# Regrouping the second norm's tiles, and placing the late lists' row numbers ahead of gates and factors

## The chip, the cores and the metric

One program runs on one core of a Trainium2 chip. The metric is the device time of an execution in microseconds (us); lower is better. Engines are named as in the profile: PE is TensorE, DVE is VectorE, ACT is ScalarE, POOL is GpSimd, SP is SyncE, which here only issues DMAs. All times in the text are from the start of the profiled execution's span.

## The reference, cut to what matters

A decoder layer over 2048 tokens of width 1024. Its last two parts are touched here. `h` is the output of the first norm:

```python
zg = xt @ w_rg + b_rg                      # 4 groups
pg = softmax(zg); gsel = argmax(zg)
ze = (xt @ w_re + b_re)[chosen group]      # 8 experts in the group
top_v, top_i = top_k(ze, 2)
gate = pg[gsel] * softmax(top_v)           # the factor of each choice
eid = gsel * 8 + top_i                     # which of 32 experts
...
hid = silu(xb @ w_gate[e]) * (xb @ w_up[e])
y  += gate * (hid @ w_down[e])             # summed per token
out = layer_norm(ALPHA * h + y, ln2_g, ln2_b)
```

## The kernel before, in words

**Stages.** A first long stage computes both mixers and merges them. The projection stage then runs over pairs of tiles (`p` from 0 to 7, two tiles of 128 tokens each): output projection on TensorE, first norm on VectorE, then routing. The expert stage goes through 32 experts in order: tokens are gathered by row number from `hd` (the normed rows in HBM), turned by TensorE, multiplied, and added to `acc` in HBM by an indirect DMA from GpSimd. Last comes the second norm, over `acc`. Instructions run on each engine in the order in which the program issues them (`manual_schedule`); an engine that waits holds everything behind it in its own queue.

**Routing of a pair.** `logits` and `gather_logits` bring the scores to PSUM through turned tiles (`hturn`). `route1` (line 1133 on) takes the maxima, makes `ef` (the expert's number), the one-hot `oh` and `ob`, and then the factor `sd` out of two sigmoids (`sp_`, `sm_`) and the gate `gt`: six small VectorE operations behind `ob`. `rank` has TensorE count, with five short matmuls, how many earlier tokens chose the same expert. `route2` makes the rank `rk` and from it `sl`, the row of an HBM table `td`; `scatter` writes token number and factor there, by four indirect DMAs of GpSimd.

**The late lists.** The last two pairs (6 and 7, `late` = 0 and 1) don't go through the table. The lists of the others are read early (`early_lists`), and the late ones are added by matmuls: `place` (line 1257) writes a one-hot `o` of the rank and, per choice, two selections `m` of the list, one with the token's number and one with its factor: twelve operations per pair, three per choice. `place_sum` multiplies `o` with both halves of `m` at once (192 columns) into one PSUM tile. The sums are added to the early lists as `TF` (row numbers) and `TG` (factors).

**Order of the hand-over** (lines 1379 to 1411, the text around the change):

```python
norm(p, (1,))              # last tile; p = 7
high(0, 2, 3); early_lists()
route2(p - 1, rank(p - 1)) # places pair 6
hturn(2 * p + 1)           # TensorE turns the last tile
logits(p, 1); gather_logits(p)
place_sum(0)
early_rows(); low(0, 2); load(2, 0, (0,))
ascale(p - 1); route1(p)
route2(p, rank(p))         # places pair 7
place_sum(1); low(0, 3); load(2, 0, (1,))
...                        # TF, TG, counts
```

`high` and `low` split a quarter of an expert's weights into a rounded and a rest part, on ScalarE and VectorE (1.2 us a piece). Behind this come `TI` (TF as integers), the first gather of expert 0's rows into `X1`, `select` (row numbers `NX` of the next blocks), the counts' register loads (`table`), the second gather, `select_last`, low(0, 4, 5), low(1, 0, 1), and `turn(X1)`: TensorE turns X1, ScalarE copies its high half, VectorE writes its low half (`bhl`). `gateup` multiplies per step high with high, high with low and low with high, so its third matmul needs VectorE's half.

**The second norm** (lines 1662 to 1769). `F` holds six groups of 2, 2, 4, 2, 4 and 2 tiles. `moments` takes a group's mean and variance on ScalarE (a summing read and a summing square per tile), `moments_v` on VectorE with its norm statistics; groups 0 and 3 go to VectorE, 1, 2, 4 and 5 to ScalarE. `root` is eleven small VectorE operations per group (a reciprocal root by Newton's steps), the first of which, `f_v`, reads the variance. `scale1` and `scale2` are one large VectorE operation each per tile. `POOL` names one tile each in groups 1 to 4 that GpSimd does whole: three operations and its own write. `weave` alternates one small operation of a group's `root` with one large one of `scale2` of the group before and `scale1` of its own.

Of the kernel before, what the change touches and what calls it, by code (L numbers as in the profile page):

```python
# [13 lines left out]
I32 = mybir.dt.int32  # L14
# [71 lines left out]
def layer(ctx, tc, a, out, dbg=None):  # L86
# [808 lines left out]
    spacer = rc_.tile([1, 1], F32, name="spacer")  # L895

    TF = rc_.tile([128, NE + 1, JB], F32, name="tf")
    TG = rc_.tile([128, NE, JB], F32, name="tg")
# [237 lines left out]
    def route1(p):  # L1136
# [27 lines left out]
        A.activation(gt[:, :, 1], dv, AF.Sigmoid, scale=-1.0)  # L1164
        ef = small("r_ef", [2, 2])
        V.tensor_copy(ef, j8[:, :, 0:2])
# [4 lines left out]
        ob = small("r_ob", [2, 32], BF16)  # L1171
        V.tensor_tensor(ob, oh[:, :, 0, :], oh[:, :, 1, :], op=OP.add)
        V.reciprocal(sm_, sm_)
        V.tensor_tensor(sp_, sp_, sm_, op=OP.mult)
# [5 lines left out]
        V.tensor_copy(sd[:, :, :, 0], tokid[:, 2 * p:2 * p + 2].unsqueeze(2).to_broadcast([128, 2, 2]))  # L1180
        RT_[p] = (ef, oh, ob, sd)

    def rank(p):
        ef, oh, ob, sd = RT_[p]
        pk = paux([128, 2, 32])
        PE.matmul(pk[:, 0, :], tri, ob[:, 0, :], start=True, stop=False)
        PE.matmul(pk[:, 0, :], onb, ohs, start=False, stop=True)
        PE.matmul(pk[:, 1, :], tri, ob[:, 1, :], start=True, stop=False)
        PE.matmul(pk[:, 1, :], onb, ob[:, 0, :], start=False, stop=False)
        PE.matmul(pk[:, 1, :], onb, ohs, start=False, stop=True)  # L1190
        return pk

    def route2(p, pk):
        ef, oh, ob, sd = RT_.pop(p)
        for t in range(2):
            V.tensor_tensor(ohs, ohs, ob[:, t, :], op=OP.add)
        V.tensor_tensor(oh, oh, pk.unsqueeze(2).to_broadcast([128, 2, 2, 32]), op=OP.mult)

        rk, sl = small("r_rk", [2, 2]), rc_.tile([128, 2, 2], I32, name="r_sl", bufs=2)
        V.tensor_reduce(rk, oh, axis=AX.X, op=OP.add)  # L1200
        dv = oh[:, :, :, 0]
        late = p - NP + 2
        if late >= 0:
            place(late, rk, ef, oh, sd)
        V.tensor_scalar(dv, rk, 1.0 / 128.0, -0.498, op0=OP.mult, op1=OP.add)
# [3 lines left out]
        V.scalar_tensor_tensor(sl, rk, 16.0, dv, op0=OP.mult, op1=OP.add)  # L1209
        if late >= 0:  # L1210
            SLD.append((sl, sd))
        else:
            scatter(sl, sd)

    SLD = []

# [15 lines left out]
    def late_buffers():  # L1232
# [11 lines left out]
        V.tensor_scalar(tv, tokid[:, NT - 4:NT], -float(EMPTY), None, op0=OP.add)  # L1244
        LB.extend([o, m, te, tf, io, tv, ps_, pmm([128, 2, NL])])

    LB = []

    def early_lists():
        te, tf = LB[2:4]  # L1250
        A.dma_start(te.rearrange("p (e c) -> p e c", e=NE), dap(td, 0, [[1024, 128], [32, NE], [1, 2 * JB]]))

    def early_rows():
        te, tf = LB[2:4]
        V.tensor_copy(tf, te.rearrange("p (n c) -> p n c", c=2)[:, :, 0])

    def place(l, rk, ef, oh, sd):
        o, m, te, tf, io, tv, ps_, pt = LB
# [8 lines left out]
        for c in range(4):  # L1267
            V.tensor_scalar(o[:, l, c], io, rm[:, c:c + 1], None, op0=OP.is_equal)
            V.tensor_scalar(m[:, l, c, 0], io[:, 0:NL], eb[:, c:c + 1], tv[:, 2 * l + c // 2:2 * l + c // 2 + 1],
                            op0=OP.is_equal, op1=OP.mult)  # L1270
            V.tensor_scalar(m[:, l, c, 1], io[:, 0:NL], eb[:, c:c + 1], sd[:, c // 2, c % 2, 1:2].bitcast(F32),
                            op0=OP.is_equal, op1=OP.mult)

    def place_sum(l):
        o, m, te, tf, io, tv, ps_, pt = LB
        for c in range(4):
            PE.matmul(pt.rearrange("p v n -> p (v n)"), o[:, l, c], m[:, l, c].rearrange("p v n -> p (v n)"),
                      start=l == 0 and c == 0, stop=l == 1 and c == 3)

# [50 lines left out]
    for p in range(NP):  # L1330
# [47 lines left out]
        if p == NP - 3:  # L1378
# [14 lines left out]
    gather_logits(p)  # L1393
    place_sum(0)
    early_rows()
    low(0, 2)
    load(2, 0, (0,))
    ascale(p - 1)
    route1(p)
    route2(p, rank(p))  # L1400
    place_sum(1)
    low(0, 3)
    load(2, 0, (1,))
    pc = paux([128, 32])
    PE.matmul(pc, onb, ohs, start=True, stop=True)
    V.tensor_tensor(TF[:, 0:NE].rearrange("p e b -> p (e b)"), LB[-1][:, 0], LB[3], op=OP.add)
    V.tensor_tensor(TG.rearrange("p e b -> p (e b)"), LB[-1][:, 1],
                    LB[2].rearrange("p (n c) -> p n c", c=2)[:, :, 1].bitcast(F32), op=OP.add)
    ascale(p)
    V.tensor_copy(cnt[:, 0:32], pc[0:1, :])  # L1410
# [170 lines left out]

    gather(X1, TI[:, 0, 0:1])
    high(1, 2, 3, 4, 5)
# [53 lines left out]
    with tc.If(mx > 128 * JB):  # L1637
        for sl, sd in SLD:
            scatter(sl, sd)
        with tc.For_i(0, NE, 1) as e:  # L1640
# [22 lines left out]
    F, i = [], 0  # L1663
    for n in (2, 2, 4, 2, 4, 2):
        f = bigt([128, n, D], F32, "f")
# [32 lines left out]

    POOL = {1: 1, 2: 3, 3: 1, 4: 3}

# [54 lines left out]

    for k in (1, 2, 4, 5):
        moments(k)
# [4 lines left out]
    weave([scale2(1)], iter(()))  # L1762
    moments_v(3)
    weave([scale1(2)], root(2))
# [27 lines left out]
```

## Time and profile before

| | us |
|---|---|
| median of 3 runs | 1833.65 (1828.17 to 1834.74) |
| the profiled execution | 1831.52 |
| its span, first to last instruction | 1829.8 |
| busy: TensorE, VectorE, ScalarE, GpSimd | 1710.9, 1324.6, 695.7, 304.9 |

The span is what the traces show; the execution's own time has 1.7 us around it. A row of a timeline gives start, duration, engine, line, operation, output and inputs with their shapes, and in brackets how long the engine had been idle before it and what ended that. Most rows have the line of a helper (L66), so the names of the tiles tell which operation it is: `late` is the buffer of `o` and `m`, `aux` a small PSUM tile, `rg` the rows of the first norm, `pt` the turned rows of a gather, `pg` the result of `gateup`.

### The profile page before, as it was taken

What the parts mean: (1) busy time and instruction counts of PE and PEld (TensorE: products, weight loads), DVE (VectorE), ACT (ScalarE), POOL (GpSimd) and SP (SyncE); (2) the same over time, 40 slices, a digit from 0 to 9 for tenths busy, and PEclk for the clock granted to TensorE, in tenths of its full rate; (3) what the DMA queues carried; (4) which work ended last, traced back from release to release, by engine and by line L of the source; (5) the groups of instructions that cost most, each with busy time, mean ns of one, the idle gap of its engine ahead of it and who ended that gap; (6) DMA issues with size and microseconds to landing.
All of it is one profiled execution on the core that took longest, in us unless ns stands there. A gap on an engine that the chain in (4) does not pass through costs nothing. (4 is left out here: it accounts for less than half of the span.)

```text
span 1829.8 us, 23985 instructions
## 1 busy us (share of the span) xinstructions
PE 1710.9 (94%) x8384; PEld 1374.7 (75%) x8385; DVE 1324.6 (72%) x2463; ACT 695.7 (38%) x1069; POOL 304.9 (17%) x304
## 2 busy tenths in 40 slices
PE   8999999999999999999999999994999999999930
PEld 7888877777777778777788888883778787887720
DVE  5798787768877875765575678898765556667748
ACT  5111221222222222633330122225776556667743
POOL 2000001101101101000000011221334333333415
PEclk9999999999999999999999999996999999999975
DMA  7321432432342325333463432546988878889855
GB/s 221 93 93 46 116 85 68 151 93 80 99 129 97 95 85 198 114 115 112 156 240 112 147 116 93 191 138 224 305 263 267 268 205 255 262 269 322 246 182 228
DMA packets 213755, 300.80 MB, mean 164 GB/s; under 512 B 29119, under 2 KB 159249, under 8 KB 211041
## 3 DMA queue, kind: packets, MB, share of 16 engines
q1 hardware_dynamic: 166496, 213.32, 35.5%
q0 software_dynamic: 22896, 56.06, 11.2%
q10 hardware_dynamic: 24208, 29.47, 4.8%
q8 instruction: 86, 1.41, 0.3%
q14 instruction: 69, 0.56, 0.1%
HBM read 224.77 MB, written 92.30 MB: 173 GB/s over the span
## 5 line engine op out<-in xcount | busy, mean ns | idle before, releaser
L66 PE MATMUL mm<-xh,whi 128*128 128x512 f32 x896 | 360.8, 403 | 0.0
L66 PE MATMUL mm<-xl,whi 128*128 128x512 f32 x896 | 353.5, 395 | 0.0
L66 PE MATMUL mm<-xh,wlo 128*128 128x512 f32 x896 | 352.1, 393 | 0.0
L66 PE MATMUL pg<-egu,bhl 128*128 128x512 f32 x1176 | 288.6, 401 | 7.8 <-DVEq L1562 7.3
L66 DVE SCALAR_TENSOR_TENSOR cvw<-cvw,cw 128x1024 f32<-128x1024 f32 x240 | 292.0, 1278 | 0.0
L66 PEld LDWEIGHTS pg<-egu,bhl 128*128 128x128 f32 x1176 | 218.3, 189 | 61.3 <-issue 5.4
L66 PEld LDWEIGHTS mm<-xh,whi 128*128 128x128 f32 x896 | 168.3, 188 | 48.0 <-ACT y L712 5.8
L66 PEld LDWEIGHTS mm<-xh,wlo 128*128 128x128 f32 x896 | 168.2, 188 | 41.5
L66 PEld LDWEIGHTS mm<-xl,whi 128*128 128x128 f32 x896 | 168.6, 188 | 36.2 <-issue 0.2
L66 PE MATMUL mm<-yt,whi 128*128 128x512 f32 x512 | 164.1, 401 | 2.1 <-ACT yt L858 1.5
L66 PE MATMUL mm<-wo,mh 128*128 128x512 f32 x512 | 162.6, 399 | 0.0
L66 DVE TENSOR_TENSOR egu<-eraw,egu 128x1024 fp32r<-128x1024 f32 x128 | 150.9, 1219 | 9.7 <-ACT egu L1313 7.0
L731 ACT ACTIVATE gt<-mm,cols 128x512 f32<-128x512 f32 x64 | 44.0, 688 | 265.4 <-PE mm L66 260.5
L1313 ACT ACTIVATE egu<-eraw 128x1024 fp32r<-128x1024 f32 x128 | 128.4, 1060 | 5.0 <-ACTq L1562 2.9
L66 PE MATMUL pd<-edn,hh 128*128 128x512 f32 x392 | 127.4, 406 | 1.0 <-ACT hh L1523 1.0
L66 PEld LDWEIGHTS mm<-yt,whi 128*128 128x128 f32 x512 | 96.6, 190 | 26.6 <-DVE yt L66 1.6
L66 PEld LDWEIGHTS mm<-wo,mh 128*128 128x128 f32 x512 | 94.2, 188 | 21.6 <-issue 1.2
L66 PE MATMUL mm<-yt,wlo 128*128 128x512 f32 x256 | 101.8, 397 | 0.0
L66 PE MATMUL mm<-wo,ml 128*128 128x512 f32 x256 | 101.0, 395 | 0.0
L66 DVE TENSOR_TENSOR edn<-erd,edn 128x1024 fp32r<-128x1024 f32 x64 | 75.7, 1224 | 27.6 <-ACT edn L1313 27.6
L1541 POOL DMA_INDIRECT acc<-yy,lq x31 | 49.8, 1606 | 228.8 <-ACT yy L1538 221.7
L66 DVE TENSOR_TENSOR hid<-hid,pg 128x256 f32<-128x256 f32 x49 | 20.4, 416 | 91.9 <-ACT hid L1515 91.9
(312 smaller groups left out, 2584.8 us busy)
## 6 DMA issues: line engine op xcount, KB each, us to landing
eraw<-in_w_gate_dram SPq DMA_DIRECT2D x64, 512.0 KB
eraw<-in_w_up_dram SPq DMA_DIRECT2D x64, 512.0 KB
erd<-in_w_down_dram SPq DMA_DIRECT2D x32, 1024.0 KB
gd<-gt ACTq DMA_DIRECT2D x64, 256.0 KB
gl<-gd SPq DMA_DIRECT2D x64, 256.0 KB
wraw<-in_w_in_dram SPq DMA_DIRECT2D x28, 512.0 KB
xt<-in_x_dram SPq DMA_DIRECT2D x16, 512.0 KB
rg<-in_x_dram SPq DMA_DIRECT2D x8, 1024.0 KB
```

Source lines behind the costliest of these rows:

```text
L66: return f(*args, **kw)
L731: A.activation(gt, p, AF.Sigmoid, bias=cols[:, BI + 12 + m:BI + 13 + m])
L1313: A.activation(h, src, AF.Copy)
L1541: G.indirect_dma_start(out=acc, out_offset=bass.IndirectOffsetOnAxis(ap=idx, axis=0), in_=y, in_offset=None, bounds_check=S - 1, oob_is_er ...
```

## The change

At the hand-over: `route1` stops at `ob`, and its six factor operations become `factors`. `place` places row numbers only, and `place_factors` the factors. `place_sum(l, v)` sums one of the two, with 96 columns into a PSUM tile of its own, and for row numbers it is called inside `route2`. `route2` also makes `TF` and `TI0` (expert 0's first column as integers) for pair 7, and adds to `ohs` only behind that. The rows of the table are no longer computed for the late pairs, except in a branch that a crowded expert would take. Then come `late_factors` (factors, their placing and their sums for both pairs), `TG`, and only then low(0, 2, 3) and load(2, 0). The first gather reads `TI0`. In the second norm the groups are 2, 2, 4, 4, 4, all but group 0 with ScalarE's sums; GpSimd's tile of group 3 is its fourth.

```diff
@@ route1, factors @@
         V.tensor_tensor(ob, oh[:, :, 0, :], oh[:, :, 1, :], op=OP.add)
+        RT_[p] = (ef, oh, ob, sp_, sm_, gt)
+
+    def factors(p, sp_, sm_, gt):
         V.reciprocal(sm_, sm_)
         V.tensor_tensor(sp_, sp_, sm_, op=OP.mult)
...
-        RT_[p] = (ef, oh, ob, sd)
+        return sd
@@ route2 @@
-        for t in range(2):
-            V.tensor_tensor(ohs, ohs, ob[:, t, :], op=OP.add)
         V.tensor_tensor(oh, oh, pk.unsqueeze(2).to_broadcast([128, 2, 2, 32]), op=OP.mult)
...
         if late >= 0:
-            place(late, rk, ef, oh, sd)
...
+            place(late, rk, ef)
+            place_sum(late, 0)
+        if late > 0:
+            lists_rows()
+        for t in range(2):
+            V.tensor_tensor(ohs, ohs, ob[:, t, :], op=OP.add)
+        if late >= 0:
+            SLD.append((late, p, rk, ef, fac))
+            return
+        sl = table_rows(rk, ef, dv)
+        scatter(sl, factors(p, *fac))
...
+    def late_factors():
+        for i, (l, p, rk, ef, fac) in enumerate(SLD):
+            sd = factors(p, *fac)
+            place_factors(l, sd)
+            place_sum(l, 1)
+            SLD[i] = rk, ef, sd
@@ lists @@
+    def lists_rows():
+        V.tensor_tensor(TF[:, 0:NE].rearrange("p e b -> p (e b)"), LB[-1][0], LB[3], op=OP.add)
+        V.tensor_copy(TI0, TF[:, 0, 0:1])
...
+    def place_factors(l, sd):
+        o, m, te, tf, io, tv, ps_, pt = LB
+        eb = ps_[:, l, 1]
+        for c in range(4):
             V.tensor_scalar(m[:, l, c, 1], io[:, 0:NL], eb[:, c:c + 1], sd[:, c // 2, c % 2, 1:2].bitcast(F32),
                             op0=OP.is_equal, op1=OP.mult)
-    def place_sum(l):
+    def place_sum(l, v):
         o, m, te, tf, io, tv, ps_, pt = LB
         for c in range(4):
-            PE.matmul(pt.rearrange("p v n -> p (v n)"), o[:, l, c], m[:, l, c].rearrange("p v n -> p (v n)"),
-                      start=l == 0 and c == 0, stop=l == 1 and c == 3)
+            PE.matmul(pt[v], o[:, l, c], m[:, l, c, v], start=l == 0 and c == 0, stop=l == 1 and c == 3)
@@ hand-over @@
     gather_logits(p)
-    place_sum(0)
     early_rows()
-    low(0, 2)
-    load(2, 0, (0,))
     ascale(p - 1)
     route1(p)
     route2(p, rank(p))
-    place_sum(1)
-    low(0, 3)
-    load(2, 0, (1,))
     pc = paux([128, 32])
     PE.matmul(pc, onb, ohs, start=True, stop=True)
-    V.tensor_tensor(TF[:, 0:NE].rearrange("p e b -> p (e b)"), LB[-1][:, 0], LB[3], op=OP.add)
-    V.tensor_tensor(TG.rearrange("p e b -> p (e b)"), LB[-1][:, 1],
+    late_factors()
+    V.tensor_tensor(TG.rearrange("p e b -> p (e b)"), LB[-1][1],
                     LB[2].rearrange("p (n c) -> p n c", c=2)[:, :, 1].bitcast(F32), op=OP.add)
+    low(0, 2, 3)
+    load(2, 0)
     ascale(p)
...
-    gather(X1, TI[:, 0, 0:1])
+    gather(X1, TI0)
@@ second norm @@
-    for n in (2, 2, 4, 2, 4, 2):
+    for n in (2, 2, 4, 4, 4):
...
-    POOL = {1: 1, 2: 3, 3: 1, 4: 3}
+    POOL = {1: 1, 2: 3, 3: 3, 4: 3}
...
-    for k in (1, 2, 4, 5):
+    for k in range(1, len(F)):
         moments(k)
...
-    moments_v(3)
     weave([scale1(2)], root(2))
```

## Rows read from the trace of the kernel before

**Rows 1.** Stretch table, expert stage: stretch, length, busy us per engine, clock, DMA.

```profile
1300.00:1400.00 100.00, 97.16 (x466) 78.58 (x465) 69.42 (x84) 70.86 (x103) 38.25 (x21) 1.00 0.92 292
```

**Rows 2.** Timeline, TensorE, hand-over: start us, us, engine, line, operation [idle before].

```profile
1245.12 1.94 PE L66 MATMUL aux<-ident,rg 128*128 128x128 f32 x8 [7.23 <-DVE ohs L66]
...
1248.90 0.92 PE L66 MATMUL aux<-pick,r_zT 128*128 128x40 f32 x4
...
1255.28 0.19 PE L66 MATMUL aux<-r_ob,tri 128*128 128x32 bf16 x1 [4.08 <-DVE r_ob L66]
...
1261.56 0.23 PE L66 MATMUL aux<-ohs,onb 128*128 128x32 bf16 x1
1269.36 1.94 PE L66 MATMUL pt<-ident,xhi 128*128 128x128 f32 x8 [7.57 <-DMA xhi<-hd,ti]
...
1272.84 7.11 PE L66 MATMUL pg<-egu,bhl 128*128 128x512 f32 x22 [0.43 <-DVE bhl L66]
```

**Rows 3.** Timeline, VectorE, hand-over.

```profile
1236.51 0.20 DVE L66 RECIPROCAL r_sm<-r_sm 128x8 f32<-128x8 f32 x1
...
1237.55 0.68 DVE L66 TENSOR_TENSOR rg<-rg,mm 128x512 f32<-128x512 f32 x1
...
1244.89 0.38 DVE L66 TENSOR_TENSOR ohs<-ohs,r_ob 128x32 bf16<-128x32 bf16 x2
...
1246.69 0.53 DVE L66 TENSOR_SCALAR late<-late 128x128 f32<-128x128 f32 x2
1247.13 0.32 DVE L66 TENSOR_SCALAR late<-late,r_sd 128x96 f32<-128x96 f32 x1
1247.37 0.52 DVE L66 TENSOR_SCALAR late<-late 128x128 f32<-128x128 f32 x2
...
1250.28 1.22 DVE L66 TENSOR_TENSOR egu<-eraw,egu 128x1024 fp32r<-128x1024 f32 x1
1251.41 0.23 DVE L66 TENSOR_TENSOR r_z<-aux,br__5889 128x80 f32<-128x80 f32 x1
...
1260.38 0.32 DVE L66 TENSOR_SCALAR late<-late,r_sd 128x96 f32<-128x96 f32 x1
...
1262.85 0.17 DVE L66 CAST cnt<-aux 1x32 int32<-1x32 f32 x1
...
1263.04 0.19 DVE L66 CAST ti<-tf 128x96 int32<-128x96 f32 x1
...
1272.10 1.28 DVE L66 TENSOR_TENSOR bhl<-pt,bhl 128x512 fp32r<-128x512 f32 x2
```

**Rows 4.** Timeline, GpSimd, hand-over: the first two gathers.

```profile
1264.21 1.06 POOL L1489 DMA_INDIRECT xhi<-hd,ti  x1 [31.84 <-DVE nx L66]
1267.72 1.94 POOL L1489 DMA_INDIRECT xhi<-hd,nx  x1 [2.45 <-DVE lq L66]
```

**Rows 5.** Timeline, VectorE, second norm.

```profile
1788.01 2.20 DVE L66 TENSOR_SCALAR f_nm<-f_mv 128x2 f32<-128x2 f32 x1
...
1795.47 1.28 DVE L66 SCALAR_TENSOR_TENSOR f<-f,f_rs,b2p 128x1024 f32<-128x1024 f32 x1
...
1823.57 2.47 DVE L66 SCALAR_TENSOR_TENSOR f<-f,f_rs,b2p 128x1024 f32<-128x1024 f32 x2
```

**Rows 6.** Timeline, ScalarE, second norm: the last sums of groups 2 and 4.

```profile
1788.38 0.19 ACT L1695 ACTIVATION_READ_ACCUMULATOR f_j<-f,f_nm 128x1 f32 x1
...
1797.44 0.18 ACT L1695 ACTIVATION_READ_ACCUMULATOR f_j<-f,f_nm 128x1 f32 x1
```

**Rows 7.** Timeline, GpSimd, second norm: one multiply, one tile's first operation and write.

```profile
1787.82 2.36 POOL L1737 TENSOR_TENSOR f<-f,eraw 128x1024 f32<-128x1024 f32 x1
...
1813.98 1.19 POOL L1735 TENSOR_SCALAR f<-f,f_nm,f_rs 128x1024 f32<-128x1024 f32 x1 [2.83 <-DVE f_v L66]
...
1820.32 0.58 POOL L1738 DMA_DIRECT2D out_dram<-f  x1 [0.30 <-POOL f L1737]
```

**Rows 8.** Instructions of the output, last line: landing of GpSimd's four writes.

```profile
DMA to landing us min/median/max: 2.9/3.0/5.1
```

More of the change, by code (lines that the diff above doesn't have):

```diff
@@ L895, in layer @@
     spacer = rc_.tile([1, 1], F32, name="spacer")
+    TI0 = rc_.tile([128, 1], I32, name="ti0")
     TF = rc_.tile([128, NE + 1, JB], F32, name="tf")
@@ L1164, in route1 @@
         A.activation(gt[:, :, 1], dv, AF.Sigmoid, scale=-1.0)
-        ef = small("r_ef", [2, 2])
+        ef = rc_.tile([128, 2, 2], F32, name="r_ef", bufs=2)
         V.tensor_copy(ef, j8[:, :, 0:2])
@@ L1180, in route1 @@
         V.tensor_copy(sd[:, :, :, 0], tokid[:, 2 * p:2 * p + 2].unsqueeze(2).to_broadcast([128, 2, 2]))
-        RT_[p] = (ef, oh, ob, sd)
+        return sd
     def rank(p):
-        ef, oh, ob, sd = RT_[p]
+        ob = RT_[p][2]
         pk = paux([128, 2, 32])
@@ L1193, in route2 @@
     def route2(p, pk):
-        ef, oh, ob, sd = RT_.pop(p)
-        for t in range(2):
-            V.tensor_tensor(ohs, ohs, ob[:, t, :], op=OP.add)
+        ef, oh, ob, *fac = RT_.pop(p)
         V.tensor_tensor(oh, oh, pk.unsqueeze(2).to_broadcast([128, 2, 2, 32]), op=OP.mult)
-        rk, sl = small("r_rk", [2, 2]), rc_.tile([128, 2, 2], I32, name="r_sl", bufs=2)
+        rk = rc_.tile([128, 2, 2], F32, name="r_rk", bufs=2)
         V.tensor_reduce(rk, oh, axis=AX.X, op=OP.add)
@@ L1203, in route2, with table_rows @@
         if late >= 0:
-            place(late, rk, ef, oh, sd)
+            place(late, rk, ef)
[9 more added lines that the diff above has]
+        scatter(sl, factors(p, *fac))
+    SLD = []
+    def late_factors():
[4 more added lines that the diff above has]
+            SLD[i] = rk, ef, sd
+    def table_rows(rk, ef, dv):
+        sl = rc_.tile([128, 2, 2], I32, name="r_sl", bufs=2)
         V.tensor_scalar(dv, rk, 1.0 / 128.0, -0.498, op0=OP.mult, op1=OP.add)
@@ L1209, in route2 @@
         V.scalar_tensor_tensor(sl, rk, 16.0, dv, op0=OP.mult, op1=OP.add)
[L1210 to L1215, printed above, removed]
+        return sl
     def scatter(sl, sd):
@@ L1244, in late_buffers @@
         V.tensor_scalar(tv, tokid[:, NT - 4:NT], -float(EMPTY), None, op0=OP.add)
-        LB.extend([o, m, te, tf, io, tv, ps_, pmm([128, 2, NL])])
+        LB.extend([o, m, te, tf, io, tv, ps_, [pmm([128, NL]) for v in range(2)]])
     LB = []
@@ L1255, in early_rows, with place @@
         V.tensor_copy(tf, te.rearrange("p (n c) -> p n c", c=2)[:, :, 0])
-    def place(l, rk, ef, oh, sd):
+    def place(l, rk, ef):
         o, m, te, tf, io, tv, ps_, pt = LB
@@ L1637, in layer @@
     with tc.If(mx > 128 * JB):
-        for sl, sd in SLD:
-            scatter(sl, sd)
+        for rk, ef, sd in SLD:
+            scatter(table_rows(rk, ef, ep.tile([128, 2, 2], F32, name="r_dv", bufs=1)), sd)
         with tc.For_i(0, NE, 1) as e:
```

## The prediction

> **What bounds the kernel now.** I read the page first (engine shares, the 40 slices), then the stretch table, then the timelines of each engine around the two edited places. The slices show TensorE at nine tenths nearly everywhere except two holes: one where routing hands over to the experts, and the end, where the second norm runs without TensorE. Between them the expert stage is TensorE's: 97.16 us busy of 100 in the stretch shown [rows 1]. So whatever is won or lost at the first hole moves the whole expert stage, and with it the end, one for one; the second hole counts directly.
>
> In the first hole TensorE's longest wait, 7.57 us, ends with the first gather's landing (X1, row 1269.36) [rows 2]. That is not the last condition, though. After the turning of X1 TensorE does two matmuls and waits again, 0.43 us, for `bhl`, VectorE's low half of X1, and goes on at 1272.84 [rows 2]. VectorE wrote that at 1272.10, straight behind its other work, with no idle time noted ahead of it nor of the other rows shown from 1236.51 on [rows 3]. Two chains therefore end together: the gather's [rows 4], and VectorE's plain sum of work, some 0.4 us later. What is won on the gather alone is worth nothing unless VectorE comes to X1 earlier too. In the second hole VectorE is busy to the last but for short waits [rows 5], ScalarE's sums run beside it [rows 6], and GpSimd does four tiles [rows 7].
>
> **The change at the hand-over, step by step.** "Pair 7" is the last two tiles, "pair 6" the two before them.
>
> *VectorE up to pair 6's placing.* The six operations of `factors` take 1.04 us (1236.51 to 1237.55) and leave this place; the same six of pair 5 move from an earlier point of the same unbroken stretch to a later one: nothing. `route2(6)` starts at 1243.85 in place of 1244.89. Its way to the first placing operation is 1.80 us (1244.89 to 1246.69), less 0.3 for the two `ohs` additions that now stand behind: 1245.35. Four pairs (rank, list) follow at 0.44 each (1246.69 to 1247.13; the factor's operation, 0.24 to 1247.37, is gone): done at 1247.2 [rows 3].
>
> *TensorE.* `place_sum(0, 0)` is now called inside `route2(6)`, so it stands in TensorE's queue ahead of the turning of the last tile, its logits and their gathering; before, it stood behind them. Each pair's matmuls wait for VectorE. The last pair's two took 0.86 us with 192 columns (VectorE's last placing operation ends at 1260.38 + 0.32, and the next matmul starts at 1261.56 [rows 2, 3]), half that with 96: 1247.6. The turning, which ran at 1245.12, runs at 1247.6. From it to the gathered logits is 4.70 us (1248.90 + 0.92) [rows 2]: 1252.3. `r_z` starts at 1252.35 and not at 1251.41: **0.9 us later**, with VectorE idle from 1247.6. Before, low(0, 2), the factor operations and table rows lay there, and hid that latency.
>
> That hold rests on TensorE keeping its order: the row at 1261.56 is a matmul on `ohs`, which VectorE had written ahead of all the placing, and it still ran behind the placing sums [rows 2]. The Trainium skill (TensorE: Matmul & The Clock Gate, Step-by-step: what each phase is for) says the same as a rule: only weight loads are pulled ahead, matmuls keep program order. By it the sum stays as here; were the turning free to overtake, it would be the second rival's.
>
> *From r_z on.* To the rank's matmuls 3.87 us as before (1251.41 to 1255.28): 1256.2; the masked ranks 0.4 later, 1256.6, no longer behind the factors. Placing 1.5 + 4 x 0.44 + 0.1: 1259.9. TensorE 0.43 and a signal: `TF` at 1260.4, `TI0` written at 1260.75, where `ti` was at 1263.23 [rows 3]. **The gather gains 2.5 us**: start 0.98 behind it (1264.21 against 1263.23), 1261.7, and X1 usable 5.15 later (1264.21 to 1269.36 [rows 2, 4]), 1266.9.
>
> *VectorE behind TI0.* All that now comes between is: `ohs` 0.3; factors twice, 2.1; eight factor placings at 0.24, 1.9; waiting for TensorE 0.45; `TG` 0.2; low(0, 2, 3), two at 1.13 (1250.28 to 1251.41), 2.3. Sum 7.2 from 1260.6: the counts are cast at 1267.8, before at 1262.85. From there to X1's low half the queue is unchanged, 9.25 us (1262.85 to 1272.10): **1277.1 instead of 1272.10, 5.0 us later** [rows 3]. X1 has then lain ready for some 8 us. In other words: VectorE gets rid of a few small operations, and waits instead for logits (4.7), rank (0.5) and two sums (0.9).
>
> *The rest.* load(2, 0)'s second half goes out some 5 us later and is read 15 us or more after that; the first half keeps its place in SP's queue. Pairs 0 to 5 scatter 1 us later, with nothing waiting: nothing; if the early lists waited for pair 5's, ScalarE had time to spare there. TensorE pauses 1.4 us longer ahead of the first expert. Its 22 matmuls took 7.11 us there [rows 2]; wholly at 1.2 GHz they would take 22 x 512 columns / 1.2 GHz = 9.4, wholly at 2.4 GHz 4.7: ends of +2.3 and -2.4. I take +0.2, nearest to the row.
>
> **The change at the end.** `moments_v(3)` goes, but VectorE wins nothing: behind scale2(1) it now waits for ScalarE's sums of group 2 (1788.57 [rows 6]), and its next operation is a small TENSOR_SCALAR like the `f_nm` of 1788.01, which took 2.20 us, until GpSimd's two-input multiply ended (1787.82 + 2.36) [rows 5, 7]. Both ways scale1(2) begins at about 1790.2.
>
> root(3) then needs ScalarE's sums of group 3, at 1797.62 [rows 6], where VectorE went on at 1795.47 before [rows 5], and GpSimd's multiply of group 2's tile holds it to 1799.2: 3.7 us lost (2.2 if it isn't held). What is won back is one root and two VectorE moments fewer. Replayed: a weave is six large operations at 1.24 [rows 5], four small ones of 0.2 (the row at 1236.51 [rows 3] is one such) that ride on nothing, and up to two holds of some 1.2; rs(3) comes at 1808.7 (ScalarE's group 4 is done at 1797.62 + 9.05 = 1806.7 [rows 6], in time), rs(4) at 1819.6. VectorE ends at 1823.3 and not 1826.04, but GpSimd's last tile starts only at 1819.8: 6.34 us to its write (1813.98 to 1820.32 [rows 7]), 1826.15, and 3.0 us to land [rows 8]: 1829.15, and the end at 1829.9 against 1829.8. **+0.1**. Ends: -2.0 if nothing is held (then ScalarE's 1806.7 sets rs(3)); +2.1 if the last write lands in 5.1 us like the slowest one [rows 8].
>
> **Sum.** 5.0 + 0.2 + 0.1 = 5.3 us. The profiled execution took 1831.52, which gives 1836.8; the median shown is 2.1 above it, which gives 1839.0; I take 1838. A measurement of this kernel can tell about 0.5% (9.2 us) from no change, so this counts as no change, on the slow side of it.
>
> **Rivals.**
> First, the gather alone sets the start, as the 7.57 us wait says. Then -2.5 us, 1831 on the median. For it: that row. Against: VectorE's row at 1272.10 and TensorE's second wait. Chance 0.08.
>
> Second, the turning of the last tile isn't held. Then it runs at 1244.1, logits at 1248.8, `r_z` at 1248.85, and X1's low half 24.75 us later: 1273.6, only +1.5, 1834 to 1835. Against: the queue order. Chance 0.13.
>
> Third, on the slow side: the gather can't start while VectorE works. Before, it started as VectorE's run paused (1264.21); after, VectorE goes on past `TI0` with two-input work until it waits for X1 itself at 1277.1. X1 would land at 1282.3 and TensorE go on 3.5 us later (1269.36 to 1272.84), at 1285.8: +12.9, 1844 to 1847. It decides if GpSimd gets no turn before 1277. Against: the gather of 1267.72 ran wholly beside VectorE's two-input work, and took 1.94 us where 1264.21's took 1.06: slowed, not shut out [rows 4]. Chance 0.07. The Trainium skill (SBUF — State Buffer, SBUF: two separate sides) speaks for it: GpSimd and VectorE hold a shared port for a whole instruction, and GpSimd's descriptors starve meanwhile. By that rule the loss could come; the row at 1267.72 shows one us.
>
> **How the numbers follow.** The forecast has 0.72, with its own range 1833 (-2.0 at the end, profiled base) to 1843 (median base, upper ends of clock or landing). The first rival reaches down to 1830.5, the third is left out above 1843.5: range 1830.5 to 1843.5. Slower by over 0.5%: the third rival, 0.07, and the forecast's upper ends together, 0.07. Faster by over 0.5% needs 9 us: no row has them to give; 0.02 for the scatter of runs.
>
> **What would show it.** Right: TensorE's transposes of the last tile behind the first placing sums, VectorE idle for 4 to 5 us ahead of `r_z`, the first gather at about 1261.7, `bhl` at about 1277 with TensorE waiting some 8 us for it, and in the tail `f_v` of group 3 ending with GpSimd's multiply, GpSimd's write last. Wrong: `r_z` no later than 1251.4, TensorE's long wait still ending with X1's gather, or an end more than 3 us off the tail's.

## The result and the profile after

The changed kernel takes 1842.05 us (median of 7 runs, 1839.35 to 1844.97), the kernel before 1831.04 beside it (7 runs): ratio 1.0062, 95% interval 1.0051 to 1.0074. It is **slower by 0.6%, 11 us**. The prediction was 1838.0: its range (to 1843.5) holds the result, but it put the loss at 5.3 us and gave no change (within 0.5%) a chance of 0.84. The profiled execution took 1843.22 us, its span is 1841.4. One execution of e1 (2482.54 us) and one of e4 (2486.23), both at a granted clock of 0.65, are left out of all that follows.

One execution reaches the hand-over a few microseconds before or after another: pair 6's `r_ob` is written at 1236.36 in the kernel before and at 1233.34 in the changed one, and over all profiles below it lies between 1233.3 and 1236.8 with either order of the rows. So I count the hand-over from that write. The row in the kernel before:

```profile
1236.36 0.22 DVE L66 TENSOR_TENSOR r_ob<-r_oh 128x64 bf16<-128x64 f32 x1
```

TensorE's timeline in the changed kernel, to be held against [rows 2]:

```profile
1242.91 2.05 PE L66 MATMUL mm<-late 128*128 128x96 f32 x8 [8.04 <-DVE late L66]
1244.76 1.91 PE L66 MATMUL aux<-ident,rg 128*128 128x128 f32 x8
...
1248.21 0.93 PE L66 MATMUL aux<-pick,r_zT 128*128 128x40 f32 x4
1253.07 0.21 PE L66 MATMUL aux<-r_ob,tri 128*128 128x32 bf16 x1 [3.92 <-DVE r_ob L66]
...
1255.43 2.05 PE L66 MATMUL mm<-late 128*128 128x96 f32 x8 [2.05 <-DVE late L66]
1258.31 0.21 PE L66 MATMUL aux<-ohs,onb 128*128 128x32 bf16 x1 [0.83 <-DVE ohs L66]
1259.91 3.89 PE L66 MATMUL mm<-late 128*128 128x96 f32 x16 [1.39 <-DVE late L66]
1268.30 1.94 PE L66 MATMUL pt<-ident,xhi 128*128 128x128 f32 x8 [4.50 <-issue]
1270.12 1.22 PE L66 MATMUL pg<-egu,bhl 128*128 128x512 f32 x2
1276.28 7.95 PE L66 MATMUL pg<-egu,bhl 128*128 128x512 f32 x22 [4.93 <-DVE bhl L66]
1284.06 1.04 PE L66 MATMUL pt<-ident,xhi 128*128 128x128 f32 x8
```

The turning of the last tile (1244.76) stands right behind the first list sums, which waited 8.04 us for VectorE. X1's turning (1268.30) no longer waits for the gather. "issue" means that the profile shows nothing it waited for; in the program TensorE loads the counts into its registers just ahead of it, and VectorE casts them only at 1266.28. In e6, below, where the turning stands ahead of the counts, there is no such wait. And the wait ahead of the 22 matmuls is now 4.93 us for `bhl`, not 0.43. VectorE's timeline at the hand-over and in the second norm [rows 3, 5]:

```profile
1233.34 0.22 DVE L66 TENSOR_TENSOR r_ob<-r_oh 128x64 bf16<-128x64 f32 x1
...
1249.18 0.24 DVE L66 TENSOR_TENSOR r_z<-aux,br__5889 128x80 f32<-128x80 f32 x1 [4.60 <-PE aux L66]
...
1257.52 0.26 DVE L66 TENSOR_TENSOR tf<-mm,late 128x96 f32<-128x96 f32 x1 [0.84 <-PE mm L66]
1257.81 0.15 DVE L66 CAST ti<-tf 128x1 int32<-128x1 f32 x1
...
1263.84 0.26 DVE L66 TENSOR_TENSOR tg<-mm,late 128x96 f32<-128x96 f32 x1 [1.39 <-PE mm L66]
1264.01 2.35 DVE L66 TENSOR_TENSOR egu<-eraw,egu 128x1024 fp32r<-128x1024 f32 x2
1266.28 0.17 DVE L66 CAST cnt<-aux 1x32 int32<-1x32 f32 x1
...
1275.54 1.28 DVE L66 TENSOR_TENSOR bhl<-pt,bhl 128x512 fp32r<-128x512 f32 x2
...
1795.93 1.35 DVE L66 TENSOR_SCALAR f_v<-f_va 128x4 f32<-128x4 f32 x1 [3.69 <-ACT f_j L1718]
...
1804.99 1.29 DVE L66 TENSOR_SCALAR f_v<-f_va 128x4 f32<-128x4 f32 x1 [2.55 <-ACT f_j L1718]
1806.19 1.27 DVE L66 SCALAR_TENSOR_TENSOR f<-f,f_rs,b2p 128x1024 f32<-128x1024 f32 x1
...
1826.67 3.67 DVE L66 SCALAR_TENSOR_TENSOR f<-f,f_rs,b2p 128x1024 f32<-128x1024 f32 x3
```

The first row is the `r_ob` from which I count. The first list sums in TensorE's queue show up as 4.60 us of idle time ahead of `r_z`. `ti` comes 24.5 us behind `r_ob` (26.7 before, 1263.04 - 1236.36), but `bhl` 42.20 us behind it (35.74 before): **the row numbers are 2.2 us earlier, X1's low half 6.5 us later.** In the second norm `f_v` of groups 3 and 4 waits 3.69 and 2.55 us for ScalarE's sums and then takes 1.35 and 1.29 us, until one of GpSimd's multiplies ends, as the prediction had it for group 3. GpSimd, at the hand-over and at the end [rows 4, 7]:

```profile
1258.78 1.06 POOL L1512 DMA_INDIRECT xhi<-hd,ti  x1 [29.74 <-DVE r_pg L66]
...
1826.82 1.18 POOL L1758 TENSOR_SCALAR f<-f,f_nm,f_rs 128x1024 f32<-128x1024 f32 x1 [3.90 <-issue]
1828.08 2.36 POOL L1759 TENSOR_TENSOR f<-f,eraw 128x1024 f32<-128x1024 f32 x1
1830.52 2.34 POOL L1760 TENSOR_TENSOR f<-f,eraw 128x1024 f32<-128x1024 f32 x1
1833.16 0.58 POOL L1761 DMA_DIRECT2D out_dram<-f  x1 [0.30 <-POOL f L1760]
```

The gather starts 0.97 behind `ti`. At the end GpSimd is last, as foreseen, with its write at 1833.16. But the span ends 8.2 us behind that, where the prediction had 3.7 (1826.15 to 1829.9). The program's closing instructions (of the last line, its waits by SyncE's queue below them) say why:

```profile
L1810 SPq EVENT_SEMAPHORE  x14: 17/28/5371, 1830.7 to 1841.4; - x14
L1810 POOLq EVENT_SEMAPHORE  x4: 17/17/17, 1840.6 to 1841.3; - x4
L1810 POOLq DRAIN  x3: 46/115/7464, 1833.1 to 1841.2; - x3
```

```profile
SPq L1810 <- DMA out_dram<-f: 5.4, 1, 5.4
SPq L1810 <- PEq L1810: 4.4, 2, 3.9
```

(The three times of an instruction are the shortest, the middle and the longest, in ns; the times behind them are the first and the last start.) The longest DRAIN on GpSimd's queue takes 7464 ns from 1833.1, and the closing events start behind it, at 1840.6. SyncE waits 5.4 us for the write to land, until 1836.8 (3.6 behind the write's start), and then another 4.4 for the other engines. The kernel before has the same DRAIN, and there nothing waits for it:

```profile
L1788 POOLq DRAIN  x3: 46/115/7463, 1820.3 to 1829.5; - x3
```

It begins at 1820.3 and ends at 1827.8. VectorE works until 1826.04, and SyncE waits for the landing of that output; the closing events start only at 1829.0.

### The profile page after: what moved, and what is told of

It reads as the page before. It is cut to its first block, busy times and chain, and to the rows that moved or that the text cites. A ratio compares the mean times of both kernels' runs of the same rounds, so it can differ in the third digit from the quotient of the medians.

```text
span 1841.4 us, 23984 instructions
## 1 busy us (share of the span) xinstructions
PE 1711.9 (93%) x8400; PEld 1378.7 (75%) x8401; DVE 1315.5 (71%) x2436; ACT 699.9 (38%) x1077; POOL 302.9 (16%) x304
## 3 DMA queue, kind: packets, MB, share of 16 engines
q1 hardware_dynamic: 166496, 213.32, 35.1%
## 5 line engine op out<-in xcount | busy, mean ns | idle before, releaser
L66 PEld LDWEIGHTS mm<-xl,whi 128*128 128x128 f32 x896 | 168.6, 188 | 36.7 <-DVE xl L66 0.5
```

The lines of the kernel that those rows point to most:

```text
L66: return f(*args, **kw)
```

## The experiments

Times are given as ratio to the kernel before on the same chip, over all executions; differences in us go by these ratios. The other columns are us, from one profile each: "bhl" (its start) and "last scatter" (the last indirect DMA into `acc`) are counted from pair 6's `r_ob`, "norm" is the first statistics operation to the end of the span.

| kernel | ratio [95%] | bhl | last scatter | norm |
|---|---|---|---|---|
| before | 1 | 35.7 | 522.6 | 59.0 |
| changed | 1.0062 [1.0051, 1.0074] | 42.2 | 532.5 | 63.5 |
| e1 norm only | 1.0022 [1.0011, 1.0032] | 35.7 | 521.2 | 63.9 |
| e2 hand-over only | 1.0029 [1.0018, 1.0040] | 42.5 | 530.2 | 59.3 |
| e3 last write by SyncE | 1.0051 [1.0037, 1.0066] | 42.4 | 532.2 | 62.0 |
| e4 sums behind logits | 1.0033 [1.0023, 1.0044] | 39.0 | 523.5 | 63.6 |
| e5 no last GpSimd tile | 1.0032 [1.0019, 1.0045] | 42.6 | 527.0 | 58.9 |
| e6 turning first | 0.9993 [0.9985, 1.0002] | 28.8 | 520.6 | 59.1 |
| e7 the same, late gather | 1.0037 [1.0022, 1.0052] | 35.1 | 526.2 | 59.4 |
| e8 residual in the wait | 1.0057 [1.0044, 1.0069] | 41.2 | 527.7 | 63.5 |
| e9 e6 with GpSimd | 1.0015 [1.0001, 1.0028] | 39.7 | 526.6 | 59.0 |
| e10 before with GpSimd | 1.0014 [1.0002, 1.0026] | 40.5 | 524.4 | 59.4 |
| e11 waits filled | 1.0004 [0.9993, 1.0014] | 36.7 | 520.5 | 59.4 |
| e12 no late table rows | 0.9986 [0.9976, 0.9995] | 34.3 | 517.8 | 59.3 |

**The two halves apart.** e1 is the kernel before with the second norm's four edits alone:

```diff
-    for n in (2, 2, 4, 2, 4, 2):
+    for n in (2, 2, 4, 4, 4):
...
-    POOL = {1: 1, 2: 3, 3: 1, 4: 3}
+    POOL = {1: 1, 2: 3, 3: 3, 4: 3}
...
-    for k in (1, 2, 4, 5):
+    for k in range(1, len(F)):
...
-    moments_v(3)
```

> The kernel before with the second norm's edit alone. Theory (the end of the program waits some 7.5 us behind GpSimd's last write for GpSimd's queue to drain, and that write now comes last): 4 to 5 us slower than the kernel before, ratio 1.0022 to 1.0027, the last GpSimd write starting about 55 us behind the first stats operation of group 0, and the end some 8 us behind that write. Rival, as predicted blind (the end is that write's landing, 3 us): +0.1 us, within 1 us of the kernel before.

Measured: ratio 1.0022, +4.0 us (2.0 to 5.9; the medians, 1833.58 and 1828.69, are 4.9 apart); GpSimd's last write at 1824.08, 55.5 behind the first statistics, the end 8.3 us behind it. The theory holds. e2 is the changed kernel with these four edits undone.

> The changed hand-over with the second norm of before. Theory (VectorE's later start of X1's low half, with TensorE's sums at half clock): 6 to 8 us slower than the kernel before, ratio 1.0033 to 1.0044, and bhl 6 to 6.5 us later than in the kernel before, counted from the same earlier operation (rg's write that follows pair 5's masked ranks). Rival A, as predicted blind: +5.2 us. Rival B (the clock's dip in the expert stage at 1348 belongs to the change): a stretch of half clock near the second expert's start shows here again, and the loss is 9 to 10 us. If the dip is chance, the clock of the stretch from 1300 to 1400 is 1.00 here and the lag is the same at 1300 and 1700 within 1 us.

Measured: 1.0029, +5.3 us (3.3 to 7.3), the two halves together 9.3 of the 11.3 that the whole ratio gives, within their intervals. `bhl` is 6.7 later, a little more than the theory has it; the time is nearest to rival A's, though the interval reaches into the theory's 6 to 8. Rival B's stretch of low clock shows here too (the clock is 0.98 from 1300 to 1400), but the loss is not its 9 to 10 us. More in the expert stage, below.

**The end of the program.** e3 changes who writes GpSimd's last tile, e5 who computes it:

```diff
e3:
-                G.dma_start(out[0, (i + t) * 128:(i + t + 1) * 128, :], f[:, t])
+                (SP if k + 1 == len(F) else G).dma_start(out[0, (i + t) * 128:(i + t + 1) * 128, :], f[:, t])
e5:
-    POOL = {1: 1, 2: 3, 3: 3, 4: 3}
+    POOL = {1: 1, 2: 3, 3: 3}
```

> The changed kernel, with the last GpSimd tile's output written by SP's queue and not by GpSimd's own. Theory (the 7.5 us belong to the drain behind GpSimd's own last write): the end comes some 3 to 3.5 us behind that write, so 4 to 5 us faster than the changed kernel, about 1837.5. Rival 1 (GpSimd's drain takes 7.5 us behind its last instruction of any kind): the same as the changed kernel, within 1 us. Rival 2 (the drain is not on the path, SP's last waits are): within 1 us of the changed kernel too, with SP's wait unchanged at over 4 us.

Measured: 1.0051, 2.0 us less than the changed kernel's 1.0062, intervals overlapping; the norm took 62.0 us, some 1.5 less. GpSimd's last lines (its timeline, then the DRAIN's row):

```profile
1823.55 0.58 POOL L1761 DMA_DIRECT2D out_dram<-f  x1 [0.30 <-DVE f_rs L66]
...
1831.73 2.34 POOL L1760 TENSOR_TENSOR f<-f,eraw 128x1024 f32<-128x1024 f32 x1
```

```profile
L1810 POOLq EVENT_SEMAPHORE  x4: 17/17/17, 1840.2 to 1840.9; - x4
L1810 POOLq DRAIN  x3: 46/115/8476, 1831.7 to 1840.7; - x3
```

The last multiply ends at 1834.07, the closing events still start only at 1840.2: 6.1 us behind an instruction that is no DMA. In the changed kernel it was 7.7 (1832.86 to 1840.6). My theory put all of it on the write; most belongs to GpSimd's end whatever came last, as rival 1 said, and some 1.6 us to the write.

> The changed kernel, with no tile of the last group given to GpSimd (VectorE does all four). Theory (GpSimd's end of program takes over 6 us behind its last instruction, so an early last instruction on GpSimd hides it): GpSimd's drain ends before the last SP write lands, VectorE ends some 2.5 us later than in the changed kernel, the end follows VectorE's last operation by 4 to 5 us in place of 11, and the kernel is 4 to 5 us faster than the changed one. Rival (the 11 us between VectorE's last operation and the end belong to the program's end whatever GpSimd does): 2 to 3 us slower than the changed kernel.

Measured: 1.0032, 5.5 us less than the changed kernel; norm 58.9. VectorE's last operation ends at 1829.16 (2.5 us more work), the span 3.9 behind it, and SyncE's waits are short again:

```profile
SPq L1810 <- DMA out_dram<-f: 1.9, 2, 1.2
SPq L1810 <- PEq L1810: 0.7, 2, 0.5
```

SyncE's long waits were thus waits for GpSimd's end, and not a cause of their own, as e3's rival 2 has it. And the norm's 4.5 us are GpSimd's late end: with that hidden, the new groups take as long as the old ones (58.9 against 59.0).

**The held turning.** e4 puts the first sums of pair 6 back behind the logits in TensorE's queue:

```diff
-            place_sum(late, 0)
+            if late > 0:
+                place_sum(late, 0)
...
     gather_logits(p)
+    place_sum(0, 0)
```

> The changed kernel with the first list sums of pair 6 behind the last tile's turning, its logits and their gathering in TensorE's queue, as before. Theory (these sums, waiting for VectorE, held the turning back): the turning starts about 3 us earlier than in the changed kernel, VectorE's idle time ahead of r_z shrinks from 4.6 to about 1.5 us, bhl comes 2.5 to 3.5 us earlier, and the kernel is about 3 us faster than the changed one, near 1839. Rival (TensorE would not have been held, the wait is for something else): r_z and bhl at the same distance from the earlier pair's masked ranks, the time unchanged within 1 us.

Measured: 1.0033, 5.3 us less than the changed kernel, where the theory has about 3. VectorE's lines:

```profile
1246.32 0.24 DVE L66 TENSOR_TENSOR r_z<-aux,br__5889 128x80 f32<-128x80 f32 x1 [1.46 <-PE aux L66]
...
1260.98 0.26 DVE L66 TENSOR_TENSOR tg<-mm,late 128x96 f32<-128x96 f32 x1 [1.40 <-PE mm L66]
...
1272.68 1.28 DVE L66 TENSOR_TENSOR bhl<-pt,bhl 128x512 fp32r<-128x512 f32 x2
```

The idle time is 1.46 us, `bhl` 39.0 behind `r_ob`, 3.2 earlier: the hold is real, and its price at `bhl` 3.2 us. That the time fell by more is not shown to come from it; in e4's profile TensorE's clock doesn't fall in the expert stage either (below). e8 leaves the hold and puts work into it:

```diff
     early_rows()
+    low(0, 2)
+    load(2, 0, (0,))
     ascale(p - 1)
...
-    low(0, 2, 3)
-    load(2, 0)
+    low(0, 3)
+    load(2, 0, (1,))
```

> The changed kernel, with the first weight residual of expert 0 (and the first half of expert 2's load behind it) back ahead of the last pair's routing, where VectorE waits 4.6 us for the logits. Theory (that wait hides it): VectorE's idle time there shrinks to about 3.5 us, bhl comes 1.1 us earlier, and the kernel is about 1 us faster than the changed one, ratio to before about 1.0055. Rival (the clock's dip near 1350, where a scatter of rows into acc lands late, comes from expert 2's load going out late): the dip is gone, the clock of the stretch from 1300 to 1400 is 1.00, and the kernel is 3 to 4 us faster than the changed one.

Measured: 1.0057, 0.9 less than the changed kernel, `bhl` 1.0 earlier: the theory, though the intervals overlap. Of the rival one half came true: the clock is 1.00 from 1300 to 1400. But the kernel is not 3 to 4 us faster, the scatter still lands late (ScalarE's wait was 3.08 us, 3.23 in the changed kernel), and the dip is as absent in e5, where the load goes out as late as in the changed kernel. So the rival's cause falls.

e11 mends both waits: e4's order, `low(0, 2)` as in e8, `low(0, 3)` ahead of `TG`, second norm as before.

> The changed hand-over mended at its two waits and nothing moved past X1: the first list sums behind the last tile's logits in TensorE's queue, one weight residual in VectorE's wait for those logits, one in its wait for the factor sums; second norm as before. Theory (these waits and the held turning are all that the change lost at the hand-over): bhl 36 to 37 us behind the anchor (35.6 in the kernel before, 38.9 with the sums moved alone), ScalarE's wait for the late scatter at 1331 to 1333 between 1.8 and 2.5 us, ratio to the kernel before 0.999 to 1.001. Rival (the expert stage loses by itself with the changed row order): bhl as early and the ratio still above 1.0015.

Measured: 1.0004 [0.9993, 1.0014], `bhl` 36.7. The loss at the hand-over is gone, and nothing is won: VectorE still waits 0.32, 0.41, 0.84 and 0.26 us for TensorE, waits that the kernel before doesn't have. ScalarE's wait was 3.08, which the theory did not expect.

**Can the early gather be used?** e6 takes e11 and moves behind X1's low half what expert 0's first matmuls don't need; e7 does the same to the kernel before, and leaves the gather late:

```diff
     gather(X1, TI0)
-    high(1, 2, 3, 4, 5)
     select()
+    gather(XN[0], NX[:, 0, 0:1])
+    turn(X1)
+    high(1, 2, 3, 4, 5)
     for e in range(2):
         table(e)
-    gather(XN[0], NX[:, 0, 0:1])
-    select_last()
+    low(1, 0, 1, 2, 3)
+    load(3, 1)
     low(0, 4, 5)
     load2(2, 0)
-    low(1, 0, 1)
-    turn(X1)
-    low(1, 2, 3, 4, 5)
-    load(3, 1)
-    load2(3, 1)
...
         turn(XN[j])
+        if e == 1:
+            low(1, 4, 5)
+            load2(3, 1)
...
             splith()
+            select_last()
```

> The early gather of the change, with VectorE's work that expert 0's first matmuls don't need (the last-block choice, the down-weight residuals, expert 1's residuals) moved behind X1's low half, TensorE's turning of X1 ahead of the count registers, the first list sums behind the last tile's logits, one weight residual in the wait for the logits and one in the wait for the factor sums; second norm as before. Theory (VectorE's sum of work up to bhl is what binds, the gather's landing next): bhl 29 to 31 us behind the last operation of the anchor (35.6 in the kernel before, 42 in the changed one), TensorE's first expert some 6 us earlier than in the kernel before; 4 to 7 us faster than the kernel before, ratio 0.996 to 0.998. Rival (the 7 us of VectorE's work that were moved come back as waits for hid and bhl in the first two experts): bhl as early, but the time within 2 us of the kernel before.

> The kernel before, with the same work of VectorE moved behind X1's low half and X1's turning ahead of the count registers, and nothing else changed: the gather is still late. Theory (two chains end within half a microsecond of each other there, so taking 7 us from VectorE's alone leaves the gather's): X1 lands where it did, bhl comes 0.5 to 1.5 us earlier, and the kernel is 0 to 1.5 us faster than before. Rival A (VectorE's sum alone set the start): 6 to 7 us faster. Rival B (the moved work is missed later): 1 to 3 us slower.

Measured: e6 0.9993 [0.9985, 1.0002], e7 1.0037. In e7 VectorE waits 7.10 us for X1 (its timeline) and `bhl` is only 0.7 earlier, as its theory says: the gather was the second chain, close behind VectorE's.

```profile
1269.95 1.50 DVE L66 TENSOR_TENSOR bhl<-pt,bhl 128x512 fp32r<-128x512 f32 x2 [7.10 <-ACT bhl L1503]
```

In e6, with the gather early, `bhl` comes 7 us earlier (28.8), yet the last scatter only 2. VectorE had no idle time over 0.6 us from 1265.6 to 1300, and then ScalarE and TensorE waited (ScalarE's timeline, TensorE's):

```profile
1331.87 0.69 ACT L1565 ACTIVATE yy<-pd,lq 128x512 f32<-128x512 f32 x1 [5.09 <-DMA acc<-yy,ll]
```

```profile
1340.64 0.41 PE L66 MATMUL ph<-ident,hid 128*128 128x128 f32 x2 [3.71 <-DVE hid L66]
...
1342.19 7.34 PE L66 MATMUL pg<-egu,bhl 128*128 128x512 f32 x24 [1.14 <-DVEq L1589]
```

So the moved work was missed later, as e6's rival and e7's rival B say. e7 is 6.8 us slower (4.0 to 9.5), more than rival B allowed; its profile shows 3.6 of them at the last scatter, the rest stays open. e9 and e10 give residuals to GpSimd (`low(..., on=G)`: six in e6's order, the four of expert 0 in the kernel before's).

> As the version with X1's turning first, but six of VectorE's weight residuals (all four of expert 0's that stand at the hand-over, and the two down-weight ones of expert 1) are done by GpSimd, which has nothing to do there. Theory (what that version won at the start it lost again by 1334, because VectorE was full from 1267 to 1318; 6.8 us of work less in that stretch keep the gain): bhl 27 to 29 us behind the anchor, the scatter rows of the expert stage still 3 to 5 us earlier than in the kernel before at 1374, and 3 to 6 us faster than the kernel before, ratio 0.9967 to 0.9984. Rival A (GpSimd's two-input work slows VectorE's beside it by as much as it takes off): VectorE's residuals beside it take 1.5 us and more where they took 1.15 to 1.2, and the time is within 2 us of the kernel before. Rival B (the expert stage's weight transfers set its pace, so an early start is lost by 1374 whatever VectorE does): bhl as early, VectorE with idle time before 1318, and the time within 2 us of the kernel before.

> The kernel before, with the four weight residuals of expert 0 that VectorE does at the hand-over done by GpSimd instead, each at its place; nothing else changed. Theory (VectorE's sum binds, the gather 0.4 us behind it): two residuals stand ahead of the row numbers, so the gather starts 1 to 2.3 us earlier, all four ahead of bhl, so bhl comes 1.5 to 2.8 us earlier, and the kernel is 1 to 3 us faster than before. Rival A (GpSimd's two-input work holds VectorE's up): VectorE's small operations beside it take over a microsecond each, and the kernel is no faster or slower. Rival B (lost again in the expert stage): bhl earlier by that much and the time within 1 us.

Measured: 1.0015 and 1.0014, 2.7 and 2.6 us slower, rival A in both. In e10 two of VectorE's residuals took 4.51 us beside GpSimd's (2.35 otherwise), but twice as much was lost on two one-column operations, 2.20 and 2.26 us in place of 0.16. (The `bhl` of e9 and e10 also holds 1.42 and 2.10 us of VectorE's waiting for the projection's matmuls behind `r_ob`, which the other profiles don't have, so GpSimd has not made all of that.) VectorE and GpSimd in e9:

```profile
1241.66 2.19 DVE L66 SCALAR_TENSOR_TENSOR n_q<-n_v,n_q 128x1 f32<-128x1 f32 x1
1243.89 2.26 DVE L66 SCALAR_TENSOR_TENSOR n_rs<-n_q,n_rs 128x1 f32<-128x1 f32 x1
...
1263.77 5.40 DVE L66 COPY r_sd<-tokid 128x4 int32<-128x4 int32 x1
```

```profile
1241.47 4.67 POOL L1346 TENSOR_TENSOR egu<-eraw,egu 128x1024 fp32r<-128x1024 f32 x2 [6.15 <-ACT egu L1341]
1263.38 1.07 POOL L1514 DMA_INDIRECT xhi<-hd,ti  x1 [17.25 <-DVE r_pg L66]
1264.48 4.65 POOL L1346 TENSOR_TENSOR edn<-erd,edn 128x1024 fp32r<-128x1024 f32 x2
```

Two one-column steps took 2.19 and 2.26 us, each to the end of one subtraction. A copy of 4 columns (0.16 us otherwise), which by the profile started during the gather ahead of them, ended only with GpSimd's two subtractions, after 5.40 us. The Trainium skill (SBUF — State Buffer, SBUF: two separate sides) says that GpSimd and a VectorE operation in a two-port mode or with two inputs in SBUF exclude each other: whichever starts first keeps the shared ports for a whole instruction while the other is blocked. The ends of these rows agree; that the copy was second to start they don't show. An operation with one input in PSUM isn't held: the row at 1806.19 of the changed kernel (`b2p` lies in PSUM) took 1.27 us beside GpSimd's multiply, and the same kind of operation 1.28 where GpSimd was idle (at 1824.69).

**A version that beats both.** e12 is the kernel before with one piece of the change: the late pairs' table rows are worked out only inside the branch that uses them.

```diff
         if late >= 0:
             place(late, rk, ef, oh, sd)
+            SLD.append((rk, ef, sd))
+            return
+        scatter(table_rows(rk, ef, dv), sd)
...
-        for sl, sd in SLD:
-            scatter(sl, sd)
+        for rk, ef, sd in SLD:
+            scatter(table_rows(rk, ef, ep.tile([128, 2, 2], F32, name="r_dv", bufs=1)), sd)
```

> The kernel before, with one of the change's savings alone: the late pairs' table rows (five small operations a pair, 0.83 us each time) are worked out only in the branch that needs them. Theory (VectorE's run binds and the gather stands behind the same operations): the gather and bhl both come 1.5 to 1.7 us earlier from the anchor, 1 to 1.7 us faster than the kernel before, ratio about 0.9992. Rival (it is lost again in the expert stage, which runs at full transfers from 1300 on): bhl earlier and the scatters at 1374 within 0.5 us of the kernel before, ratio 1.000.

Measured: 1826.22 against 1828.79, ratio **0.9986 [0.9976, 0.9995], 2.6 us faster**. TensorE:

```profile
1266.80 1.94 PE L66 MATMUL pt<-ident,xhi 128*128 128x128 f32 x8 [7.79 <-DMA xhi<-hd,ti]
1268.62 7.06 PE L66 MATMUL pg<-egu,bhl 128*128 128x512 f32 x24
```

The gather starts (26.4 behind `r_ob`, 27.9 before) and `bhl` comes 1.4 us earlier, X1 can be turned 0.5 earlier, and the first expert's 24 matmuls run without the second wait. The rival falls: the ninth scatter starts 2.5 us earlier than in the kernel before (134.3 behind `r_ob`, 136.8 before). The gain is 2.6 us where 1 to 1.7 were expected, and its interval, 0.9 to 4.4, holds the theory.

**The expert stage.** In the changed kernel ScalarE waits at 1337 for an earlier scatter into `acc`, TensorE then for `hid`, and the next 24 matmuls run long:

```profile
1337.44 0.69 ACT L1561 ACTIVATE yy<-pd,lq 128x512 f32<-128x512 f32 x1 [3.23 <-DMA acc<-yy,ll]
```

```profile
1346.21 0.41 PE L66 MATMUL ph<-ident,hid 128*128 128x128 f32 x2 [1.86 <-DVE hid L66]
1347.66 8.56 PE L66 MATMUL pg<-egu,bhl 128*128 128x512 f32 x24 [1.04 <-DVEq L1585]
```

The first of these rows in the kernel before:

```profile
1332.15 0.69 ACT L1538 ACTIVATE yy<-pd,lq 128x512 f32<-128x512 f32 x1 [1.82 <-DMA acc<-yy,ll]
```

There TensorE's wait for `hid` is 0.35 us, and the matmuls take 5.84. The granted clock of the changed kernel is 0.84 from 1340 to 1350 and 0.82 from 1350 to 1360, and 1.00 before 1346 and behind 1354. Over the profiles: with the kernel before's own list order and nothing moved past X1 (before, e1, e10, e12) ScalarE's wait is 1.75 to 2.06; with the change's order (changed, e2 to e5, e8, e9, e11) 2.45 to 3.24. TensorE waited 1.07 to 1.86 there, and then the clock fell to half (1.2 GHz) for a few microseconds in the changed kernel, e2, e3 and e9 (24 matmuls in 7.3 to 8.6 us), and not in e4, e5, e8 and e11 (5.8). With work moved past X1 it fell in e6 (a wait of 3.71) and not in e7 (2.09). e2, e3 and e5 have the same hand-over as the changed kernel: the wait belongs to it, the fall of the clock is not in every execution. What makes that scatter land later stays open. Expert 2's load going out late doesn't (e8 for its first half, e11 for both), nor does a late start: e11 starts 0.9 late and waits 3.08, e10, with the old order, starts 4.8 late and waits 1.93. From the ninth scatter (1373.2 in the kernel before) to the last, the kernel before and e1 take 385.7 and 386.2 us, the others 382.1 to 385.3: 0.4 to 4 us come back there, by a way that I haven't followed.

## Why the prediction held its range and missed the size

- **The range held in part by luck.** Its upper end was counted up from 1833.65, the median of 3 runs that stood there; over the 7 runs the kernel before takes 1831.04, and from that base the same end would lie at 1840.9, below the result. The upper ends of clock and landing that it allowed for did not come; what filled their room was a term that the sum didn't have (the last point).
- **What binds: right.** Two chains close together, VectorE's sum the later (e7: 0.7 us); e12 shortens both and gains, the change shortened one and lengthened the other.
- **The held turning: right**, shown by e4, and the second rival (not held) falls with it. `r_z` came 15.8 us behind `r_ob` (16.0 predicted, 1252.35 - 1236.36), after 4.60 us of idle time (4.7 predicted).
- **The gather: right.** `ti` is written 24.6 us behind `r_ob` (24.4 predicted, 1260.75 - 1236.36), and the gather starts 25.4 behind it (25.3 predicted). The first rival (gather alone decides) and the third (gather shut out) are refuted by the rows.
- **VectorE behind `TI0`: under-sized.** 5.0 us became 6.5 (6.5 to 6.9 in the four profiles with this hand-over). I took 0.45 for each wait for TensorE's sums; they were 0.84 and 1.39. I had halved the time of two wider matmuls of the kernel before. But the 16 factor sums run 3.89 us in a row and so end 1.4 behind VectorE's last placing, and the clock granted there was 0.56 (1250 to 1260) and 0.50 (1260 to 1270).
- **TensorE's registers: not seen.** X1's turning waited 4.50 us for the counts, which now come late. It cost nothing, since `bhl` was later still.
- **The clock in the first expert: +0.2 predicted, +0.8 here** (7.95 us for 22 matmuls against 7.11), within the ends given. The profiles scatter, but the change has a part in it as far as they show: the four with this hand-over took 6.85 to 8.13, e1, with the unchanged one, 5.41.
- **"One for one": wrong, in both directions.** The prediction carried the hand-over's loss unchanged to the end. The four profiles with this hand-over are 6.5 to 6.9 us late at `bhl` and 4.4 to 9.9 at the last scatter: they wait up to 1.9 us at 1346, some have a half-speed stretch behind it, and some time comes back later. That e2's +5.3 agrees with the +5.2 of the sum is therefore luck at least in part: at `bhl` alone it was 6.7. How the pieces add up to 5.3 is not shown. e6 shows the same for a gain: 7 us early, 2 us at the last scatter, 1.3 in the time, which can't be told from none.
- **The second norm: the step that failed.** Up to the last instruction the replay was right: GpSimd's last write 55.3 us behind the first statistics (55.35 predicted), VectorE's end 52.5 (52.5 predicted). The last step was wrong, 3.0 us for that write to land and the end at 1829.9: the term of +0.1 measured +4.0 (2.0 to 5.9), more than the 3 us that the prediction had named as its sign of being wrong. I took the landing of a write [rows 8] for the end of the program, and did not read the closing DRAIN, which stood in the trace of before at 7463 ns, hidden behind VectorE. With that row read (8.2 us from the last write to the end in place of 3.7) the sum would have been about +9.8 and the call "slower".

## What to carry to other kernels

When a change makes another engine the last to finish, read the closing instructions of the trace, not only the last data transfer: a wait of several microseconds can lie hidden there behind the engine that was last before. When two chains end together, count what a reordering does to both; the cheap win was to take work out of the run that both share (e12), not to pull one chain forward. And a helper engine is free only if its operations leave the other's alone: look at the smallest instructions beside it as well as the large ones.

## What the runs showed of the hardware

In this kernel GpSimd's closing DRAIN lasts 7.46 us from the issue of its last write, or 6.1 us from the end of a last multiply whose result goes out through another queue (e3). A two-input subtraction on GpSimd (2.35 us) holds up VectorE's small operations in SBUF until it ends: 2.2 us instead of 0.16, and 5.40 with two in a row; an operation with one input in PSUM ran beside GpSimd's multiply in 1.27. The granted clock of TensorE fell to half in the middle of the expert stage after waits of 1.1 to 1.9 and 1.0 to 1.2 us in four profiles, for 3 to 7 us, and stayed at full after waits of 1.1 to 2.1 and 1.0 to 1.2 us in five others.
